# Loads for whole steps, one tile for a step's operands, and resident tiles of L in a layer of attention and RWKV-7 time mixing

## The chip, the cores and the metric

One core of a Trainium2 chip runs the whole layer. The metric is the device time of one launch in microseconds (us), the median of three runs. Engines are named as in the profile: PE (matrix engine), PEld (its weight load), DVE (vector), ACT (scalar), POOL (GpSimd), SP (the queue that issues every DMA here).

## The reference, cut to what matters

The layer normalises and modulates x, projects it once, gives half of the columns to eight heads of two-dimensional neighbourhood attention and half to eight heads of a bidirectional RWKV-7 recurrence, joins the two through an output projection, and ends in a SwiGLU feed-forward part. The recurrence is what the change touches:

```python
def wkv_scan(s0, r, w, k, v, a, b, reverse):
    '''S <- S diag(w) + (S a) b^T + v k^T ;  y = S r.'''
    def step(s, inp):
        r_t, w_t, k_t, v_t, a_t, b_t = inp
        sa = jnp.einsum('bhvk,bhk->bhv', s, a_t)
        s = s * w_t[:, :, None, :] + sa[..., None] * b_t[:, :, None, :] + v_t[..., None] * k_t[:, :, None, :]
        return s, jnp.einsum('bhvk,bhk->bhv', s, r_t)
...
    for d, rev in enumerate((False, True)):
        s_ctx, y_c = wkv_scan(s0, *ic, reverse=rev)
        _, y_x = wkv_scan(s_ctx, *ix, reverse=rev)
        wkv = wkv + y_x
...
        mix = jnp.concatenate([o_na, o_rw.astype(h.dtype)], axis=-1) @ w_out[l]
```

There are 2048 latent tokens in rows of 64, 256 context tokens, a width of 1024, and heads of 64.

## The kernel before

The program has three stages: projections (to about 895 us of the span), then the stage of this change, `phase2`, with the recurrence and the attention side by side (to about 1887 us), then the output projection (first matmul at L1458) and the feed-forward part.

**The recurrence in chunks.** The 2304 tokens are cut into 18 steps s of 128 tokens, each of two chunks of 64, so there are 36 chunks m = 2s + c. A chunk is worked for both directions and for four pairs of heads (hp or q) at once. Its operands (decayed keys, receptances and so on) were written to the DRAM tensor `d_b` by the stage before. Four kinds of work make a chunk ready:

- A *build* (L1004 to L1015), one per step and pair, loads `ga` and `bk`, multiplies them on PE, and copies or masks the product into `lx` (ACT, L1010), `ga` (DVE, L1011) and `gb` (DVE, L1015). `lx` holds the triangular matrices L.
- An *inverse*, one per two steps (a pair of steps, G = s // 2), inverts the triangles in `lx`. It is a long run of DVE operations on one tile (L1057 to L1089), then small matmuls and copies (L1104 to L1117).
- A *late* loads `bkl` and transposes it (L1028 to L1039), per chunk.
- A *load of v* fills `zv` (L1130), per chunk.

The *chain* then takes the chunks one after the other, since each needs the state z of the one before: copies of z into `zv` (L1175, L1176), matmuls with `ga` (L1185), a copy (L1189), matmuls with the inverted `lx` (L1195), copies (L1198, L1199), matmuls with `tt` (L1205), the new state on DVE (L1210, then L1225), and beside it the output y (L1218, L1222, L1230, stored to `d_y`).

**Attention** is 64 tiles: scores (L740), maxima and exponentials (L775 to L784, DVE and ACT), transposes (L790, L793), products (L829), a transpose back (L836) and the scaled output `ot` (L839). It shares no data with the recurrence.

**What sets the order.** Builds, inverses, lates, chain, attention and some preparation are generators ("streams"). `emit` merges them: it keeps a clock for each engine and always takes the piece that could start first, with the offsets of `LATE` (the tiles of attention come 60 us late, that is, last). The pieces say with "wait" and "post" what they need, and with "get" and "put" who holds the two PSUM banks that builds, lates, inverses and some of the preparation share. A scheduler then orders all instructions once more. Every engine, and SP, runs its instructions in the order that results.

**The waits that matter.** A build of pair G waits until the chain has done step 2G - 3, the last step of pair G - 2, since the tiles of `lx` come from two pools of one tile each. There are 16 units of `ga` and `gb`, one for each step and pair of heads, in a ring, so a build also waits for the step four before it. The inverse of G waits for the eight builds of steps 2G and 2G + 1, and the chain's step 2G waits for that inverse.

Of the kernel before, what the change touches and what calls it, by code (L numbers as in the profile page):

```python
# [19 lines left out]
P = 128  # L20
# [826 lines left out]
NU = 16  # L847
SHIFT = 1
# [9 lines left out]
LATE = (0, 0, -10, -10, 0, 0, 0, 60, 0)  # L858
# [3 lines left out]
def emit(banks, *streams):  # L862
# [4 lines left out]
    free, when = {}, {}  # L867
# [44 lines left out]
def phase2(k):  # L912
# [4 lines left out]
    with ExitStack() as ctx:  # L917
# [36 lines left out]
        U, LX, ZV, TT_ = {}, {}, {}, {}  # L954
# [4 lines left out]
        for i in range(NU):  # L959
            u = K()  # L960
            u.ga = un[i].tile([P, 3, 4, 64], F32, name=f"ga{i}")
            u.gb = un[i].tile([P, 2, 4, 64], F32, name=f"gb{i}")
# [8 lines left out]
        def build(s, hp, w):  # L971

            G, j0 = s // 2, 4 * (s % 2)
            u = units[(4 * s + hp + SHIFT) % NU]
# [4 lines left out]
            if G not in LX:  # L979
                LX[G] = lp[G % 2].tile([P, 4, 8, 64], F32, tag="lx", name="lx")  # L980
            lx = LX[G]
            U[s, hp] = u
            src = k.d_b[hp, s]
            for h in range(2):
                if s > 1:
                    nc.sync.dma_start(out=u.ga[H[h], h:3:2 - h], in_=src[H[h], 0:512].rearrange(
                        "p (x j t) -> p x j t", x=2, j=4))
                else:
                    nc.sync.dma_start(out=u.ga[H[h], h], in_=src[H[h], 0:256].rearrange("p (j t) -> p j t", j=4))
            bk = bp.tile([P, 4, 128], F32, tag=f"bk{w}", name="bk", bufs=2)  # L990
            nc.sync.dma_start(out=bk, in_=src[:, 512:1024].rearrange("p (j t) -> p j t", j=4))
            yield "run", ("DMA", 3.0)
# [8 lines left out]
            for j in range(4):  # L1001
                for h in range(2):
                    with run.next():
                        run.last = nc.tensor.matmul(gp[h][:, j, 0:N], bk[H[h], j], u.ga[H[h], h:3:2 - h, j, :] if s > 1  # L1004
                                                    else u.ga[H[h], h, j, :], start=True, stop=True).ins
            dc = "p (d c) t -> p d c t"
            for h in range(2):
# [3 lines left out]
                nc.vector.tensor_tensor(u.ga[ko, h].rearrange(dc, d=2), gp[h][ko, :, 0:64].rearrange(dc, d=2),  # L1011
                                        maskS[ko, :, None, :].to_broadcast([64, 2, 2, 64]), op=ALU.mult)
                if s > 1:
                    yield "run", ("DVE", -0.34)
                    nc.vector.tensor_tensor(u.gb[:, h].rearrange(dc, d=2), gp[h][:, :, 64:128].rearrange(dc, d=2),  # L1015
# [4 lines left out]
        def lates(g):  # L1020

            for m in range(2 * NS):
# [3 lines left out]
                bk = bl.tile([P, 2, 2, P], F32, tag="bkl", name="bkl")  # L1026
                for q in range(2):
# [3 lines left out]
                z = []  # L1031
                yield "get", z, 1
                yield "run", ("PE", 0.45)
                for q in range(2):
                    for dd in range(2):
                        nc.tensor.transpose(z[0][:, (2 * q + dd) * P:(2 * q + dd + 1) * P], bk[:, q, dd], k.ident)
                tt = TT_[m, g] = tp.tile([P, 2, 2, P], F32, tag=f"tt{g}", name="tt", bufs=2)
                yield "run", ("ACT", -0.52)
                nc.scalar.activation(tt.rearrange("p q d x -> p (q d x)"), z[0], AF.Copy)  # L1039
                yield "put", z[0]  # L1040
                yield "post", ("late", m, g)

        def inverses():
# [3 lines left out]
            for s in range(NS // 2):  # L1047
                yield ("wait",) + tuple(("built", 2 * s + e, hp) for e in range(2) for hp in range(4))
                lx = LX[s]
# [23 lines left out]
                for q in range(4, 32, 4):  # L1073

                    m, n = q, 32 - q
                    yield "run", ("DVE", 0.25 + 8 * m * n / 960)
# [45 lines left out]
        def load_v(m):  # L1122
# [3 lines left out]

            for h in range(2):
                for dd in range(2):
                    t0 = toks(s)[dd] + 64 * (1 - c if dd else c)
                    nc.sync.dma_start(out=zv[H[1 - h], h, dd, :], in_=k.d_vs[t0:t0 + 64, 256 * h:256 * h + 256])  # L1130
# [13 lines left out]
        def chains():  # L1144
# [5 lines left out]
            for s in range(NS):  # L1150
                yield "wait", ("inv", s // 2, 3)
                us = [U.pop((s, hp)) for hp in range(4)]
                for c in range(2):
                    m = 2 * s + c
                    yield "wait", ("late", m, 0), ("late", m, 1)
                    if m + 1 < 2 * NS:
                        load_v(m + 1)
                    z = yield from chain(s, c, z, us)
# [5 lines left out]
        def chain(s, c, z, us):  # L1164
            lx, j0 = LX[s // 2], 4 * (s % 2)
            zv = ZV[2 * s + c]
            tt = [TT_.pop((2 * s + c, g)) for g in range(2)]
# [14 lines left out]
            for i, (dd, q) in enumerate(dq):  # L1182
                for h in range(2):
                    with run.next():
                        run.last = nc.tensor.matmul(rp[H[h], i, :], us[q].ga[:, h, 2 * dd + c, :], slot(h, dd, q),  # L1185
# [522 lines left out]
```

## Time and profile before

| | |
|---|---|
| median of three runs | 3523.22 us (3523.1 to 3530.65) |
| profiled execution | 3522.23 us, its span 3520.5 us |
| mean granted clock of PE | 0.950 |
| PE busy over the span | 3239.0 us (92%) |
| DVE busy | 2396.8 us (68%) |
| ACT busy | 1465.8 us (42%) |

The shares are averages over three stages. Times in the text are microseconds from the start of the span of the profiled execution. Positions of the chain are given by the DVE operation at L1210, the new state z of a chunk: there are 36 of them, numbered from 0. The granted clock is a share of the full 2.4 GHz; 1.2 GHz is the other level.

### The profile page before, as it was taken

Reading aid. Unit: us, or ns where it says so; the run is one execution under the profiler, and the core shown is the slowest. Engines: PE = TensorE matmul, PEld = TensorE weight load, DVE = VectorE, ACT = ScalarE, POOL = GpSimd, SP = SyncE. Lnnn points to the kernel's source line nnn. Section 1 sums busy time; section 2 is a strip of 40 time slices with the busy share of each in tenths; the row PEclk is TensorE's granted clock in tenths of the full one; section 3 lists DMA queues with packets and bytes.
Section 4 is the critical chain, followed back from the end, with each engine's and each line's share of the span. In section 5 each row is a group of like instructions: output and inputs, shape, how many; then the busy total and the mean of one; then the engine's idle time right before and its main releaser. Section 6 shows DMA issues by size and latency. Waiting matters only on the chain. (4 is left out here: it accounts for less than half of the span.)

```text
span 3520.5 us, 66352 instructions
## 1 busy us (share of the span) xinstructions
PE 3239.0 (92%) x25202; PEld 2775.8 (79%) x25202; DVE 2396.8 (68%) x4489; ACT 1465.8 (42%) x3186; POOL 1101.2 (31%) x1057
## 2 busy tenths in 40 slices
PE   7899999999879889798856999999899999999999
PEld 5787878789657677576655887888799998899998
DVE  7758786774385766847655754444877778777776
ACT  4524343442445556465433553233333334333332
POOL 3425543453000100100113433333433334433332
PEclk9999999999888899899877999999999999999999
DMA  7546666553634446354326554332422223422222
GB/s 244 160 140 198 189 193 199 160 172 113 194 105 130 142 126 196 97 166 126 87 78 189 183 174 159 96 102 84 150 63 72 67 72 102 135 72 72 66 64 69
DMA packets 461856, 458.50 MB, mean 130 GB/s; under 512 B 56656, under 2 KB 381664, under 8 KB 461536
## 3 DMA queue, kind: packets, MB, share of 16 engines
q1 hardware_dynamic: 461536, 454.25, 42.7%
q8 instruction: 199, 3.26, 0.4%
q14 instruction: 121, 0.99, 0.1%
HBM read 346.37 MB, written 107.75 MB: 129 GB/s over the span
## 5 line engine op out<-in xcount | busy, mean ns | idle before, releaser
L1329 ACT ACTIVATE w<-raw 128x512 fp32r<-128x512 f32 x440 | 270.9, 627 | 497.8 <-PE acc L1618 190.2
L1538 PE MATMUL acc<-ua,w 128*128 128x384 f32 x2464 | 469.8, 336 | 6.0 <-POOL w L1330 2.7
L1618 PE MATMUL acc<-w,fh 128*128 128x512 f32 x1408 | 435.7, 394 | 18.7 <-ACT fh L1329 7.3
L1330 DVE TENSOR_TENSOR w<-raw,w 128x512 fp32r<-128x512 f32 x308 | 273.3, 891 | 247.0 <-ACT w L1329 120.0
L1538 PEld LDWEIGHTS acc<-ua,w 128*128 128x128 f32 x2464 | 433.2, 189 | 9.9 <-POOL w L1330 4.2
L219 PE MATMUL acc<-u,wh 128*128 128x512 f32 (+3 forms) x1120 | 347.9, 390 | 11.4 <-DVE sh L257 6.7
L1618 PEld LDWEIGHTS acc<-w,fh 128*128 128x128 f32 x1408 | 266.4, 190 | 79.4 <-ACT fh L1329 9.1
L503 PE MATMUL acc<-wt,u 128*128 128x256 f32 x2496 | 321.1, 287 | 5.0 <-DVE sh L257 2.3
L503 PEld LDWEIGHTS acc<-wt,u 128*128 128x128 f32 x2496 | 307.9, 194 | 12.3 <-issue 4.6
L1609 POOL TENSOR_TENSOR raw<-raw,gate 128x512 f32<-128x512 f32 x132 | 179.3, 1369 | 409.8 <-DMA raw<-in_w_dram 354.1
L1330 POOL TENSOR_TENSOR w<-raw,w 128x512 fp32r<-128x512 f32 x132 | 186.2, 1411 | 272.0 <-PE acc L1538 57.6
L1618 PE MATMUL acc<-w,fl 128*128 128x512 f32 x704 | 269.4, 392 | 0.1
L1538 PE MATMUL acc<-ux,w 128*128 128x384 f32 x1232 | 252.1, 335 | 0.3 <-DVE w L1330 0.3
L219 PEld LDWEIGHTS acc<-u,wh 128*128 128x128 f32 (+1 forms) x1120 | 206.0, 191 | 58.5 <-issue 7.0
L1520 PE MATMUL acc<-ua,w 128*128 128x512 f32 x1056 | 241.7, 389 | 2.0 <-POOL w L1330 1.1
L1520 PEld LDWEIGHTS acc<-ua,w 128*128 128x128 f32 x1056 | 198.0, 188 | 43.7 <-POOL w L1330 1.6
L219 PE MATMUL acc<-u,wl 128*128 128x512 f32 (+3 forms) x560 | 218.0, 389 | 2.8 <-DVE wl L210 2.7
L1538 PEld LDWEIGHTS acc<-ux,w 128*128 128x128 f32 x1232 | 216.8, 188 | 1.6 <-DVE w L1330 1.0
L1623 DVE TENSOR_TENSOR h<-h,acc 128x512 f32<-128x512 f32 x192 | 126.3, 683 | 100.3 <-PE acc L1618 100.1
L1179 POOL COPY zp<-z 64x512 f32<-64x512 f32 x64 | 41.4, 647 | 453.4 <-PE up L1218 293.7
L1330 POOL TENSOR_TENSOR w<-s,w 128x512 fp32r<-128x512 f32 x88 | 131.6, 1496 | 152.5 <-PE acc L1538 56.6
L1530 DVE TENSOR_TENSOR t<-acc,t 128x384 f32<-128x384 f32 x308 | 169.7, 551 | 13.9 <-PE acc L1538 7.3
(256 smaller groups left out, 6728.9 us busy)
## 6 DMA issues: line engine op xcount, KB each, us to landing
raw<-in_w_dram SPq DMA_DIRECT2D x132, 512.0 KB
raw<-in_w_dram SPq DMA_DIRECT2D x132, 256.0 KB
wada<-in_w_ada_dram SPq DMA_DIRECT2D x96, 256.0 KB
d_b<-bk SPq DMA_DIRECT2D x72, 256.0 KB
bkl<-d_b SPq DMA_DIRECT2D x144, 128.0 KB
bk<-d_b SPq DMA_DIRECT2D x72, 256.0 KB
d_b<-ar SPq DMA_DIRECT2D x136, 128.0 KB
xt<-in_x_dram SPq DMA_DIRECT2D x32, 512.0 KB
```

The lines of the kernel that those rows point to most:

```text
L219: nc.tensor.matmul(acc[:m, :n], a_[:, kk % 4, :m], b_[b][:, kk, :], start=(i == 0), stop=(i == 23))
L503: nc.tensor.matmul(acc[:, 256 * e:256 * e + 256], a_[b][:, kk, (j + e) * P:(j + e + 1) * P], ws[kk][:, h, :], start=(i == 0), stop=(i == 23))
L1179: nc.gpsimd.tensor_copy(zp[H[h], h], z[H[h]])
L1329: nc.scalar.activation(hl[0], v, AF.Copy)
L1330: eng.tensor_tensor(hl[1], v, hl[0].bitcast(F32), op=sub)
L1520: nc.tensor.matmul(acc, hl[wi][:, kk, :], u[ui][:, 4 * hf + kk, :], start=q == 0, stop=q == 23)
L1530: vadd = lambda o, x, y: nc.vector.tensor_tensor(o, x, y, op=add)
L1538: nc.tensor.matmul(acc, w[wi][:, kk, :], u[i][ui][:, kk, :], start=q == 0, stop=q == 11)
L1609: nc.gpsimd.tensor_tensor(raw, raw, g2[:, o], op=ALU.mult)
L1618: nc.tensor.matmul(acc, a_[:, f, ts], w2[f][:, hl, :], start=(i == 0), stop=(i == 6 * np_ - 1))
L1623: nc.vector.tensor_tensor(hs[j][:, o], hs[j][:, o], acc, op=add)
```

## The change

All of it is in `phase2` and `emit`.

- There are 4 units in place of 16, each for a whole step (all four pairs): `ga` is [128, 4, 3, 4, 64], `gb` is [128, 4, 2, 4, 64].
- A stream of builds loads for two pairs at a time: four DMAs for `ga` and one for `bk`, in place of four and two. The tile `bk` holds two pairs and has one buffer per stream (before, one pair and two buffers). The streams take pairs 0, 1 and 2, 3 (before 0, 2 and 1, 3).
- The two tiles of `lx` are made once and stay. The wait for step 2G - 3 is gone from the builds; what is left is the wait for step s - 4, before the loads of step s. So the first step of a pair can be built a step of the chain earlier; the second step still waits for 2G - 3.
- One stream of lates in place of two: two DMAs per chunk, each with all four pairs of one direction, in place of four; the two groups of transposes follow in turn.
- `zv` takes two DMAs per chunk, each with both directions, in place of four.
- In `emit`, a request for banks is served in the order in which it was made. The pieces of an inverse's DVE work are announced in larger blocks.

The number of instructions on PE, DVE, ACT and POOL is the same. There are 1963 DMAs in place of 2151. Lines of after are 1 to 6 higher than those of before for the same operation (L1057 is L1059, L1210 is L1216, L1225 is L1231, L1176 is L1182, L1458 is L1464); those of attention are unchanged.

```diff
-NU = 16
-SHIFT = 1
+NU = 4
-LATE = (0, 0, -10, -10, 0, 0, 0, 60, 0)
+LATE = (0, 0, -10, 0, 0, 0, 60, 0)
...
-                elif op == "get" and len(banks) >= args[1]:
+                elif op == "get" and e not in asked:
+                    asked.append(e)
+                    continue
+                elif op == "get" and asked[0] is e and len(banks) >= args[1]:
+                    asked.pop(0)
...
+        LX = [lp[i].tile([P, 4, 8, 64], F32, name=f"lx{i}") for i in range(2)]
...
             for s in range(NS):
-                for hp in (w, w + 2):
-                    yield from build(s, hp, w)
+                if s >= NU:
+                    yield "wait", ("chain", s - NU)
+                u = units[s % NU]
+                qs = slice(2 * w, 2 * w + 2)
+                src = k.d_b[qs, s]
+                for h in range(2):
+                    for x in range(2 if s > 1 else 1):
+                        nc.sync.dma_start(out=u.ga[H[h], qs, 2 if x else h].rearrange("p q j t -> p q (j t)"),
+                                          in_=src[:, H[h], 256 * x:256 * x + 256].rearrange("q p y -> p q y"))
+                bk = bp.tile([P, 2, 4, 128], F32, tag=f"bk{w}", name="bk")
+                nc.sync.dma_start(out=bk.rearrange("p q j t -> p q (j t)"),
+                                  in_=src[:, :, 512:1024].rearrange("q p y -> p q y"))
+                yield "run", ("DMA", 3.0)
+                for q in range(2):
+                    yield from build(s, 2 * w + q, u.ga[:, 2 * w + q], u.gb[:, 2 * w + q], bk[:, q])
...
-            if G > 1:
-                yield "wait", ("chain", 2 * G - 3)
-            if 4 * s + hp >= NU:
-                yield "wait", ("chain", (4 * s + hp - NU) // 4)
...
-                    nc.sync.dma_start(out=bk[:, q], in_=k.d_b[2 * g + q, s, :, 512:1024].rearrange(
-                        "p (d c x) -> c p d x", d=2, c=2)[c])
+                    nc.sync.dma_start(out=bk[:, :, dd], in_=k.d_b[:, s, :, x0:x0 + P].rearrange("q p x -> p q x"))
...
+                    if q % 2:
+                        yield "run", ("DVE", 1.0 if q == 1 else 4.2)
                     for i in range(q):
-                        yield "run", ("DVE", 0.5)
...
-                for dd in range(2):
-                    t0 = toks(s)[dd] + 64 * (1 - c if dd else c)
-                    nc.sync.dma_start(out=zv[H[1 - h], h, dd, :], in_=k.d_vs[t0:t0 + 64, 256 * h:256 * h + 256])
+                z = zv[H[1 - h], h]
+                nc.sync.dma_start(out=z if n0 < n1 else z[:, ::-1], in_=v[:, :, 256 * h:256 * h + 256])
...
-        emit(banks, chains(), inverses(), lates(0), lates(1), builds(0), builds(1), at.products(), at.tiles(),
+        emit(banks, chains(), inverses(), lates(), builds(0), builds(1), at.products(), at.tiles(),
```

**What it does to the order.** On DVE before, a middle inverse (G = 4; L1057 is its first operation) begins among builds and attention. At this place 16 chunks of the chain and 38 tiles of attention are done; no operation of the chain (L1176, L1199, L1210, L1225) stands on DVE between here and the inverse's last copy (L1117).

```order
L1011 TENSOR_TENSOR ga_9766<-bank_9724,maskS 64x256
L1015 TENSOR_TENSOR gb_9767<-bank_9724,maskI 128x256
L1057 STREAM_TRANSPOSE lu<-lx 128x32x32
L839 TENSOR_TENSOR ot<-sx_9781,st 128x128
L775 TENSOR_REDUCE st<-sx_9781 128x1
L1011 TENSOR_TENSOR ga_9764<-bank_9725,maskS 64x256
L1015 TENSOR_TENSOR gb_9765<-bank_9725,maskI 128x256
L1011 TENSOR_TENSOR ga_9764<-bank_9724,maskS 64x256
L1070 TENSOR_TENSOR xtmp<-lu 128x256
```

On DVE after, a middle inverse (G = 5; L1059 is its first operation) has the chain's operations (L1216 and L1231 the new state, L1182 the copy for the next chunk) among its own (L1073, L1075).

```order
L1059 STREAM_TRANSPOSE lu<-lx_9709 128x32x32
L1216 TENSOR_TENSOR z_15240<-rp,z_15010 128x512
L776 ISA pr,st<-sw_9720,es 128x384
L776 ISA st 128x1
L1231 TENSOR_TENSOR z_15240<-z_15240,pc 128x512
L778 TENSOR_SCALAR st<-st 128x1
L1073 TENSOR_TENSOR xtmp<-lu 128x256
L1182 COPY zv<-z_15240 64x512
L1075 TENSOR_TENSOR lu<-lu,xtmp 128x8x32
```

Between the two, chunks of the chain moved into the inverse: of the chunks done at the first and the last DVE operation of an inverse, before shows 8 and 8, 8 and 11, 16 and 16, 16 and 18, 24 and 24, 24 and 27, 32 and 32 for G = 2 to 8, and after 6 and 8, 9 and 12, 13 and 16, 17 and 20, 22 and 24, 25 and 28, 29 and 32.

On PE before, the chain's last matmuls (L1218, L1222, the output y) stand right ahead of the output projection (L1416 transposes its input, L1458 is its matmul); attention has ended long before.

```order
L1218 MATMUL up<-zp,ga_9758 64x64 x2
L1222 MATMUL up<-zv,gb_9759 64x64 x2
L1218 MATMUL up<-zp,ga_9760 64x64 x2
L1222 MATMUL up<-zv,gb_9761 64x64 x2
L1416 MATMUL mtp<-ident,mx 128x128 x4
L1458 MATMUL acc<-wo_20857,mh 128x512 x4
```

On PE after, the last rows ahead of the output projection (L1464) are those of attention (L793, L790, L829, L836); L1422 is the transposition of its input, L1285 a matmul of the time mixing's gate.

```order
L793 MATMUL sw_9721<-ident,pr 128x128 x3
L790 MATMUL sx_9722<-ident,pr 128x128 x2
L1422 MATMUL mtp<-ident,mx 128x128 x4
L836 MATMUL sx_9723<-ident,oT 128x128
L829 MATMUL sx_9722<-pr,vw 64x128 x6
L829 MATMUL sx_9722<-pr,vc 64x128 x4
L836 MATMUL sx_9723<-ident,oT 128x128
L1285 MATMUL g<-gup,gd 128x512
L1464 MATMUL acc<-wo_20482,mh 128x512 x3
```

The end of the chain moved ahead of the end of attention: after, 57 of the 64 outputs `ot` of attention stand ahead of the chain's last state z on DVE, before all 64.

On SP before, among the loads for a step are the two halves of `ga` (L986) of one pair each; L1028 loads half of a late.

```order
L1028 DMA bkl<-d_b 128x2x128 x2
L986 DMA ga_9750<-d_b 64x2x256
L986 DMA ga_9750<-d_b 64x512
L986 DMA ga_9752<-d_b 64x2x256
L986 DMA ga_9752<-d_b 64x512
```

On SP after, a load of `bk` (L984) or of `ga` (L981) carries two pairs, one of a late (L1030) four pairs, one of `zv` (L1136) both directions; `sg` is attention's.

```order
L1136 DMA zv<-d_vs 64x2x256 x2
L984 DMA bk<-d_b 128x2x512
L981 DMA ga_9710<-d_b 64x2x256 x2
L1030 DMA bkl<-d_b 128x4x128
L698 DMA sg<-d_k 128x8x128
L700 DMA sg<-d_q 128x4x128
L1030 DMA bkl<-d_b 128x4x128
```

The loads became fewer and larger, with the same bytes.

## Rows read from the trace of the kernel before

**Rows 1.** Windows: length, busy of PE, PEld, DVE, ACT, POOL, clock, DMA share, GB/s.
```profile
971.00:1091.00 120.00, 94.72 (x1293) 72.04 (x1289) 90.72 (x207) 53.38 (x139) 8.39 (x8) 0.78 0.36 102
1091.00:1786.00 695.00, 603.98 (x9313) 484.39 (x9311) 462.38 (x1182) 388.88 (x1027) 68.58 (x86) 0.91 0.48 136
1166.00:1249.00 83.00, 64.48 (x755) 47.56 (x750) 63.95 (x163) 41.17 (x115) 8.95 (x8) 0.86 0.38 109
1249.00:1382.00 133.00, 123.37 (x2130) 101.78 (x2130) 83.18 (x217) 84.65 (x223) 12.11 (x18) 0.95 0.59 164
1382.00:1464.00 82.00, 62.34 (x716) 47.93 (x715) 65.41 (x164) 38.94 (x107) 8.55 (x8) 0.84 0.40 117
```

**Rows 2.** Timeline of DVE: start, duration, operation; first inverse, states z, an inverse.
```profile
971.19 2.13 DVE L1057 STREAM_TRANSPOSE lu<-lx 128x1024 f32<-128x1024 f32 x1
...
1091.22 0.69 DVE L1210 TENSOR_TENSOR z<-rp,z 128x512 f32<-128x512 f32 x1 [1.47 <-PE rp L1205]
...
1302.48 0.69 DVE L1210 TENSOR_TENSOR z<-rp,z 128x512 f32<-128x512 f32 x1 [1.80 <-PE rp L1205]
...
1397.07 2.12 DVE L1057 STREAM_TRANSPOSE lu<-lx 128x1024 f32<-128x1024 f32 x1
...
1455.02 0.69 DVE L1117 COPY lx<-bank 32x512 f32<-32x512 f32 x1
...
1520.10 0.69 DVE L1210 TENSOR_TENSOR z<-rp,z 128x512 f32<-128x512 f32 x1 [1.22 <-PE rp L1205]
...
1785.60 0.67 DVE L1210 TENSOR_TENSOR z<-rp,z 128x512 f32<-128x512 f32 x1
```

**Rows 3.** Timeline of PE: first builds of steps 0, 8 and 9; the output projection begins.
```profile
909.36 0.69 PE L1004 MATMUL bank<-ga,bk 64*128 64x64 f32 x2
...
1310.44 0.83 PE L1004 MATMUL bank<-ga,bk 64*128 64x128 f32 x10
...
1349.91 1.16 PE L1004 MATMUL bank<-ga,bk 64*128 64x128 f32 x16
...
1886.91 1.08 PE L1416 MATMUL mtp<-ident,mx 128*128 128x128 f32 x4 [11.45 <-DMA mx<-d_mix]
1888.68 1.22 PE L1458 MATMUL acc<-wo,mh 128*128 128x512 f32 x2 [0.69 <-ACT mh L1329]
```

**Rows 4.** Groups of DVE, 1040 to 1834: count, busy, mean ns, idle before.
```profile
L1199 DVE COPY zv<-up 64x512 f32<-64x512 f32 x32 | 22.2, 695 | 26.9 <-ACT zv L1198 26.1
L1225 DVE TENSOR_TENSOR z<-z,pc 128x512 f32<-128x512 f32 x32 | 22.0, 687 | 0.4
L1210 DVE TENSOR_TENSOR z<-rp,z 128x512 f32<-128x512 f32 x32 | 21.9, 684 | 21.4 <-PE rp L1205 21.4
...
L1176 DVE COPY zv<-z 64x512 f32<-64x512 f32 x32 | 16.0, 500 | 1.0
```

**Rows 5.** Groups of PE that are attention's, 1091 to 1786, columns as in rows 4.
```profile
L740 PE MATMUL sw<-ks,q 64*128 64x384 f32 (+1 forms) x200 | 76.2, 618 | 1.9 <-ACT pr L798 1.8
L740 PE MATMUL sx<-kc,q 64*128 64x256 f32 x198 | 69.5, 433 | 2.0 <-ACT pr L796 2.0
...
L793 PE MATMUL sw<-ident,pr 128*128 128x128 f32 x348 | 60.4, 299 | 12.9 <-ACT pr L784 12.5
L829 PE MATMUL sx<-pr,vw 128*64 128x128 f32 x708 | 56.9, 288 | 8.3 <-ACT pr L782 4.1 <-DVE st L775 3.4 <-ACT pr L796 0.6
...
L790 PE MATMUL sx<-ident,pr 128*128 128x128 f32 x200 | 40.7, 307 | 3.6 <-ACT pr L782 3.3
...
L829 PE MATMUL sx<-pr,vc 128*64 128x128 f32 x408 | 36.6, 278 | 0.0
...
L836 PE MATMUL sx<-ident,oT 128*128 128x128 f32 x51 | 16.4, 321 | 2.7 <-ACT oT L834 2.6
```

**Rows 6.** Loads of the lates: issue time in ns, and who waited (us, times).
```profile
L1028 SPq DMA_DIRECT2D bkl<-d_b x144: 354/468/1443, 859.0 to 1832.0; - x144
...
  PE bank L1036: 13.4, 8
```

More of the change, by code (lines that the diff above doesn't have):

```diff
@@ L967, in builds, with build @@
             for s in range(NS):
-                for hp in (w, w + 2):
-                    yield from build(s, hp, w)
-        def build(s, hp, w):
-            G, j0 = s // 2, 4 * (s % 2)
-            u = units[(4 * s + hp + SHIFT) % NU]
-            if G > 1:
-                yield "wait", ("chain", 2 * G - 3)
-            if 4 * s + hp >= NU:
-                yield "wait", ("chain", (4 * s + hp - NU) // 4)
[L979 to L992, printed above, removed]
+                if s >= NU:
[13 more added lines that the diff above has]
+                    yield from build(s, 2 * w + q, u.ga[:, 2 * w + q], u.gb[:, 2 * w + q], bk[:, q])
+        def build(s, hp, ga, gb, bk):
+            G, j0 = s // 2, 4 * (s % 2)
+            lx = LX[G % 2]
             N = 128 if s > 1 else 64
@@ L1075, in inverses @@
                     m, n = q, 32 - q
-                    yield "run", ("DVE", 0.25 + 8 * m * n / 960)
+                    if q % 8 == 4:
+                        yield "run", ("DVE", sum(0.25 + 8 * r * (32 - r) / 960 for r in (q, q + 4) if r < 32))
                     tv = tmp[:, :4 * m * n].rearrange("p (c a b) -> p a c b", c=4, a=m)
@@ L1151, in chains @@
                 yield "wait", ("inv", s // 2, 3)
-                us = [U.pop((s, hp)) for hp in range(4)]
+                u = units[s % NU]
                 for c in range(2):
                     m = 2 * s + c
-                    yield "wait", ("late", m, 0), ("late", m, 1)
+                    yield "wait", ("late", m)
                     if m + 1 < 2 * NS:
                         load_v(m + 1)
-                    z = yield from chain(s, c, z, us)
+                    z = yield from chain(s, c, z, u)
                     yield "post", ("chunk", m)
@@ L1162, in phase2, with chain @@
         dq = [(dd, q) for dd in range(2) for q in range(4)]
-        def chain(s, c, z, us):
-            lx, j0 = LX[s // 2], 4 * (s % 2)
+        def chain(s, c, z, u):
+            lx, j0 = LX[s // 2 % 2], 4 * (s % 2)
             zv = ZV[2 * s + c]
-            tt = [TT_.pop((2 * s + c, g)) for g in range(2)]
+            tt = TT_.pop(2 * s + c)
             zf = z.rearrange("p d q n -> p d (q n)")
@@ L1184, in chain @@
                     with run.next():
-                        run.last = nc.tensor.matmul(rp[H[h], i, :], us[q].ga[:, h, 2 * dd + c, :], slot(h, dd, q),
+                        run.last = nc.tensor.matmul(rp[H[h], i, :], u.ga[:, q, h, 2 * dd + c, :], slot(h, dd, q),
                                                     start=True, stop=True).ins
@@ L1204, in chain @@
                     with run.next():
-                        run.last = nc.tensor.matmul(rp[H[h], i, :], tt[q // 2][:, q % 2, dd, H[h]], slot(h, dd, q),
+                        run.last = nc.tensor.matmul(rp[H[h], i, :], tt[:, q, dd, H[h]], slot(h, dd, q),
                                                     start=True, stop=True).ins
@@ L1217, in chain @@
                         with run.next():
[L1218 removed]
+                            run.last = nc.tensor.matmul(up_[H[h], i, :], u.ga[:, q, 2, 2 * dd + c, :],
                                                         zp[:, h, dd, q, :], start=True, stop=False).ins
@@ L1221, in chain @@
                         with run.next():
-                            run.last = nc.tensor.matmul(up_[H[h], i, :], us[q].gb[:, h, 2 * dd + c, :],
+                            run.last = nc.tensor.matmul(up_[H[h], i, :], u.gb[:, q, h, 2 * dd + c, :],
                                                         slot(h, dd, q), start=False, stop=True).ins
```

52 lines of the change are left out of this document (28 added, 24 removed).

## The prediction

> **What bounds the kernel now.** The change touches one stage, so I read that stage alone, first by its windows, then by the position of the chain. From the state z of chunk 3 at 1091.22 us to that of chunk 31 at 1785.60 us [rows 2] the stage is in its steady course: PE is busy 603.98 of 695 us (87%), DVE 462.38 (67%), ACT 388.88 (56%) [rows 1]. No engine is full, and yet nothing idles for long. The three windows behind it in that group show why: the course swings between two conditions. From 1249 to 1382 PE is busy 123.37 of 133 us (93%) and DVE 83.18 (63%). Just before it and just after it, in 1166 to 1249 and 1382 to 1464, PE is at 78% and 76%, DVE at 77% and 80%, and the granted clock falls from 0.95 to 0.86 and 0.84. These are the stretches in which the chain stands and two inverses run one behind the other on DVE.
>
> The chain shows the loop that makes them. The state of chunk 11 (end of step 5) comes at 1302.48. Only then may builds of steps 8 and 9 begin; on PE they start at 1310.44 and 1349.91 [rows 3]. The inverse of that pair starts on DVE at 1397.07 and its last copy begins at 1455.02 [rows 2]. So 94.6 us pass from the chain to the inverse, 58.6 in the inverse (to the end of its 0.69 us copy), and four chunks then run in 64.4, until 1520.10. The sum is 217.6 us for eight chunks. From 1091.22 to 1785.60 there are 28 chunks in 694.4 us, or 99.2 us for four. I call the time of four chunks p.
>
> **The change part by part.** The sum is made against the profiled execution, 3522.2 us, which lies 1.0 under the median.
>
> *Start, to the state of chunk 3.* After, all eight builds of the first two steps stand ahead of attention's first scores, so inverse 0 needs only them. Before, the first build is at 909.36 [rows 3] and the inverse begins at 971.19 [rows 2]. Sixteen matmul records of a build, all it has, lie within 1.16 us on PE [rows 3], and with the turn of two banks through ACT and DVE I estimate 3 us for each, 24 for eight; a first build at about 903 and 8 us to the inverse's first operation give 935, or 36 earlier. But what stands on DVE from there to the state of chunk 3 grows: by counts of the order times the mean durations of before, from 101 to 119 us. At the packing of 971 to 1091, where DVE is busy 90.72 of 120 us [rows 1], that is 120 × 119 / 101 = 141, so 21 are given back. **Net 15 gained**, with bounds 0 and 30.
>
> *Steady course, 28 chunks: 7p.* The loop gets shorter by the first of its two steps of builds, since the first step of a pair now waits for step 2G - 4: 94.6 less the 39.5 between 1310.44 and 1349.91 [rows 3] leaves 55.1. The inverse gets longer, as three chunks of the chain now run within it: four DVE operations of 0.695, 0.687, 0.684 and 0.500 us [rows 4] are 2.57 us a chunk, 7.7 for three, so 66.3. With 64.4 for four free chunks the eight take 185.8, so p = 93. From the other side, PE: 603.98 us of work done at a clock of 0.91, of which the part in the two standing stretches ran at 0.84 to 0.86. At 0.95 those would shrink by a tenth, and over the whole I take 590. At the 93% of the best window that is 634, or p = 91. **I take p = 92**, 644 us in place of 694.4: 50 gained. For this, PE and DVE must be busy together for (590 + 462) / 644 = 163% of the time, where the three windows show 155, 155 and 156% and the whole 153%. This is what I trust least: bounds are p = 86 (PE shrinks to 565 at 94%) and 99.2 (no better packing).
>
> *End, from the state of chunk 31 to the output projection.* Before this is 1785.60 to 1888.68 [rows 2, 3], 103.1 us: inverse 8 and four chunks alone, without attention, which is done. After, about 18 us of inverse 8's DVE work is left at that point, which I put at 19 us, then come four chunks with five tiles of attention, at the pace of four free chunks, 65. Then seven tiles of attention are left alone. On PE a tile costs at least 7.1 us: the seven groups sum to 356.7 over the 50 tiles of that window (200 sw records, four to a tile) [rows 5]. At most it costs 13.9, the 695 us of the window by 50. Alone it is nearer to the first; I take 8, so 56 us. The idle 11.45 us of PE for the last input [rows 3] is covered, since time mixing of the first tiles now lies beside attention, but the splits of the output weights come after the last tile, which I put at 4 us, under those 11.45. Together 144, **41 lost**, with bounds 28 and 82.
>
> *Loads.* 188 DMAs fewer, with an issue of 0.468 us for one of a late [rows 6], are some 88 us of SP. SP is not what others wait for: PE waited 13.4 us in all for such loads [rows 6]. One load for two pairs with a single `bk` buffer comes later than one for a pair, and the loads of the second step of a pair still start only when the chain is through. Bounds are 13 gained and, if each of the seven pairs waits 4 us longer, 28 lost; I take 0, since the lates and `zv` have chunks of lead. The Trainium skill ("DMA: Bandwidth & Descriptors", Rules for kernel authors) says to coalesce many small transfers; its section on the anatomy of one DMA gives about 2.0 us fixed for each on another path than this one. By that, an estimate from the page, 188 would be 376 us and the time 3122 if they lay on the path; rows 6 speak against that. The same rules say that two transfers to disjoint partition halves serialize, which speaks against the halves that `ga` and `zv` keep; no row here separates that.
>
> *FIFO of the banks, larger blocks, fewer units.* They only move the order, and that is counted above. Instruction counts of the four computing engines do not change.
>
> The sum: 15 + (694.4 - 7p) - 41 = 668 - 7p. With p = 92 it is 24 us gained: **3522.2 - 24 = 3498 us**, 3499 against the median. A measurement here can tell about 0.3%, 10.6 us, from no change. So the change is faster below p = 94.0, the same to 97.0, and slower above.
>
> **The rivals.**
>
> *Better packing.* With the inverses beside the chain nothing stands, PE stays at its 93% or above and the clock at 0.95. For it: the 1249 to 1382 window held that for 133 us, with DVE at 63%. Against it: DVE must carry 77% at the same time, which no PE-bound window here shows. At p = 86 the gain is 66, 3456 us.
>
> *No change.* p = 95.5, so that the end's 41 us eat the middle: 3522. It happens if DVE, at 77 to 80% in the standing stretches, keeps the chain's operations waiting about 1 us a chunk more than I took, or if the later loads cost their 4 us a pair.
>
> *Slower: the inverse in the chain's way.* DVE runs in order. In an inverse of after, an operation of the chain stands behind a run of inverse operations, and PE and ACT, which have the chunk's next matmuls and copies in their own order, stand behind it with attention's work queued up. Before, the chain simply stood there and attention filled PE. If each of three chunks waits 2 us at each of its three hops to DVE, 18 us, the loop is 203.8 for eight chunks, p = 102, and the time is 3522 - 668 + 714 = 3568. If the pace merely stays at 99.2, the end alone makes it 3548. From p = 97 it decides. For it: 21.4 and 26.9 us of DVE idle before L1210 and L1199 [rows 4] show that these hops wait on PE and ACT, so a shift at one comes out at the others. Against it: the chain has few DVE operations, and work beside it fills in.
>
> *The change doesn't do what it says.* The order shows the chain's rows inside the inverses, so this is left with next to nothing.
>
> **How the numbers follow.** I give the forecast (p from 88 to 94) 0.45, better packing (p under 88) 0.15, no change 0.17, slower 0.23. So faster by over 0.3% is 0.60, within 0.3% is 0.17, slower by over 0.3% is 0.23. The range leaves out about 2 in 10: below, p = 86 with 4 us of the other bounds, 3452; above, p = 99.2 to 99.5, 3550. The likeliest case alone reaches from 3470 to 3512.
>
> **What would show it right or wrong.** In the profile after: the first inverse (L1059) at about 935; the state of chunk 3 (L1216) near 1076; from there to chunk 31 some 644 us, with PE near 90%, DVE near 72% and a clock that no longer dips to 0.85; no stretch of 70 us in which the chain stands; about 144 us from chunk 31 to the first L1464, with some 56 us at a lower clock that only attention fills. If 28 chunks take over 680 us, packing was the wrong step; if the end takes over 160, the tiles alone were sized wrongly; if PE waits for `bk` or `ga` from DMA for over 20 us, the loads were.

## The result and the profile after

The changed kernel takes 3493.83 us (median of six, 3486.9 to 3511.09) against 3524.22 (3521.88 to 3532.28) for the kernel before beside it: a ratio of 0.9915, with a 95% interval of 0.9895 to 0.9936. It is faster by 30 us; the forecast was 3498 us. The profiled executions are 3492.62 and 3522.23 us, 29.6 apart. The landmarks of after that answer to [rows 2] and [rows 3] are these, from the timelines of DVE and PE (start, duration, operation): the first inverse, states z of chunks 3, 11, 15, 19, 23, 31 and 35 (L1216), two middle inverses (L1059 to L1121) and the last one's end, the first build and the first output projection.

```profile
932.67 2.12 DVE L1059 STREAM_TRANSPOSE lu<-lx 128x1024 f32<-128x1024 f32 x1
...
1072.80 0.67 DVE L1216 TENSOR_TENSOR z<-rp,z 128x512 f32<-128x512 f32 x1
...
1244.25 0.68 DVE L1216 TENSOR_TENSOR z<-rp,z 128x512 f32<-128x512 f32 x1
...
1300.69 2.08 DVE L1059 STREAM_TRANSPOSE lu<-lx 128x1024 f32<-128x1024 f32 x1
...
1352.26 0.69 DVE L1216 TENSOR_TENSOR z<-rp,z 128x512 f32<-128x512 f32 x1
...
1366.86 0.69 DVE L1121 COPY lx<-bank 32x512 f32<-32x512 f32 x1
...
1393.36 2.15 DVE L1059 STREAM_TRANSPOSE lu<-lx 128x1024 f32<-128x1024 f32 x1
...
1433.58 0.69 DVE L1216 TENSOR_TENSOR z<-rp,z 128x512 f32<-128x512 f32 x1 [1.57 <-PE rp L1211]
...
1471.20 0.69 DVE L1121 COPY lx<-bank 32x512 f32<-32x512 f32 x1 [2.47 <-ACT lx L1121]
...
1535.39 0.69 DVE L1216 TENSOR_TENSOR z<-rp,z 128x512 f32<-128x512 f32 x1 [0.71 <-PE rp L1211]
...
1728.48 0.68 DVE L1216 TENSOR_TENSOR z<-rp,z 128x512 f32<-128x512 f32 x1
...
1751.83 0.69 DVE L1121 COPY lx<-bank 32x512 f32<-32x512 f32 x1 [0.74 <-ACT lx L1121]
...
1803.67 0.69 DVE L1216 TENSOR_TENSOR z<-rp,z 128x512 f32<-128x512 f32 x1 [0.98 <-PE rp L1211]
```

```profile
890.50 0.43 PE L1005 MATMUL bank<-ga,bk 64*128 64x64 f32 x2
...
1856.06 1.03 PE L1285 MATMUL g<-gup,gd 128*128 128x512 f32 x2
1856.84 0.73 PE L1464 MATMUL acc<-wo,mh 128*128 128x512 f32 x2
```

The windows (columns as in [rows 1]) of the steady course, of one inverse within it, and of the attention that is left behind the chain:

```profile
1072.80:1728.50 655.70, 580.13 (x8993) 464.09 (x8992) 459.37 (x1125) 356.12 (x922) 74.57 (x89) 0.90 0.51 141
...
1393.00:1472.00 79.00, 65.17 (x1008) 51.73 (x1004) 54.21 (x129) 37.54 (x101) 7.16 (x9) 0.83 0.52 143
...
1804.00:1857.00 53.00, 41.92 (x326) 26.78 (x323) 28.16 (x87) 28.71 (x86) 15.17 (x12) 0.90 0.50 155
```

Read term by term against [rows 2, 3]:

| stretch | before | after | gained | forecast |
|---|---|---|---|---|
| to the state of chunk 3 | 1091.2 | 1072.8 | 18.4 | 15 |
| 28 chunks, to chunk 31 | 694.4 | 655.7 | 38.7 | 50 |
| chunk 31 to the output projection | 103.1 | 128.4 | -25.3 | -41 |
| the rest | 1631.8 | 1634.1 | -2.3 | 0 |

So the three terms have the sign and roughly the size of the sum, and their errors (3 us of gain too little, 11 too much, 16 of loss too much) cancel to 5 us, which is luck. Work also moved between the stretches: of the 64 tiles of attention, before does 13 ahead of the state of chunk 3 and 51 in the 28 chunks; after does 8 and 44, and the other 12 after chunk 31, five of them beside the last four chunks and seven alone. So a term that shrank may only have handed on its work. The change also moves the wait, the order of the banks, the blocks of an inverse and the loads at once. The experiments take them apart.

### The profile page after: what moved, and what is told of

The parts are those of the page before. It is cut to its first block, busy times and chain, and to the rows that moved or that the text cites. A ratio compares the mean times of both kernels' runs of the same rounds, so it can differ in the third digit from the quotient of the medians.

```text
span 3490.9 us, 66140 instructions
## 1 busy us (share of the span) xinstructions
PE 3265.8 (94%) x25202; PEld 2788.0 (80%) x25202; DVE 2396.7 (69%) x4489; ACT 1466.9 (42%) x3186; POOL 1107.7 (32%) x1057
## 5 line engine op out<-in xcount | busy, mean ns | idle before, releaser
L1544 PEld LDWEIGHTS acc<-ux,w 128*128 128x128 f32 x1232 | 216.8, 188 | 3.0 <-POOL w L1336 1.5
```

The lines of the kernel that those rows point to most:

```text
L1544: nc.tensor.matmul(acc, w[wi][:, kk, :], u[i][ui][:, kk, :], start=q == 0, stop=q == 11)
```

## The experiments

Three theories stood at the start: A, the loop is shorter because the wait for step 2G - 3 is gone (the prediction's); B, the new order of the requests for banks does it; C, the fewer DMAs do it. Ratios are always to the kernel before on the same chip. "28 chunks" runs from the state z of chunk 3 to that of chunk 31, the "end" from there to the first output projection, both in the one profiled execution. The tiles are outputs `ot` of attention on DVE within the 28 chunks, of 64 in all; before has 51 there, after 44.

| label | what it is | median us | ratio (95%) | 28 chunks, tiles | end |
|---|---|---|---|---|---|
| e1_wait_back | after, old wait | 3502.24 | 0.9914 (0.9888 to 0.9941) | 701.5, 52 | 98.4 |
| e2_small_loads | after, small loads | 3490.77 | 0.9878 (0.9860 to 0.9897) | 652.8, 44 | 130.4 |
| e3_banks_as_before | after, old bank order and blocks | 3502.65 | 0.9910 (0.9888 to 0.9932) | 684.3, 50 | 90.3 |
| e4_resident_L_alone | before, resident L, no wait | 3485.46 | 0.9866 (0.9844 to 0.9888) | 654.2, 50 | 95.5 |
| e5_changed_again | after | 3500.85 | 0.9915 (0.9899 to 0.9931) | 650.8, 44 | 133.7 |
| e6_resident_L_again | as e4 | 3486.03 | 0.9870 (0.9848 to 0.9892) | 659.1, 50 | 97.2 |
| e7_bank_order_alone | before, new bank order | 3494.44 | 0.9895 (0.9877 to 0.9914) | 701.2, 53 | 105.4 |
| e8_small_blocks | after, small blocks | 3469.79 | 0.9836 (0.9810 to 0.9862) | 669.0, 48 | 92.9 |
| e9_small_blocks_again | as e8 | 3470.46 | 0.9831 (0.9811 to 0.9852) | 670.7, 48 | 95.4 |
| e10_small_blocks_small_loads | e8 with small loads | 3465.14 | 0.9815 (0.9792 to 0.9837) | 666.8, 48 | 98.7 |
| e11_large_loads_alone | before, new loads, units and lates | 3517.16 | 0.9961 (0.9947 to 0.9975) | 687.7, 51 | 102.7 |
| e12_resident_L_large_blocks | e4 with large blocks | 3502.86 | 0.9915 (0.9890 to 0.9939) | 691.5, 47 | 83.4 |

Kernels e1 to e4 ran beside each other, e5 to e8, and e9 to e12; the kernel before had medians of 3536.33, 3530.95 and 3530.95 there.

**The old wait back in the changed kernel.**

```diff
                 if s >= NU:
-                    yield "wait", ("chain", s - NU)
+                    yield "wait", ("chain", s // 2 * 2 - 3)
```

> The changed kernel with the old wait put back: the loads and builds of both steps of a pair G wait for the chain's step 2G - 3 again. Theory A (my prediction: the loop is shorter because the first step of a pair is built a step earlier): the 28 chunks from chunk 3 to chunk 31 go back from 656 us towards 694, and the time to 3515 or above. Theory B (the gain comes from the order in which the two shared banks are given out, which lets inverses and chain run side by side): the 28 chunks stay under 675 us and the time between 3475 and 3500; the order shows all 64 tiles of attention ahead of the chain's last state, so the end is short. Theory C (fewer and larger DMAs): 3494 as in the changed kernel.

The middle is as long as theory A says: 701.5 us where after needs 655.7. Its window, and the timeline of the same execution at the states of chunks 3 and 31 and at the output projection:

```profile
1074.50:1776.00 701.50, 635.72 (x9444) 503.94 (x9442) 477.71 (x1221) 404.76 (x1057) 72.16 (x89) 0.91 0.51 141
```

```profile
1074.53 0.69 DVE L1216 TENSOR_TENSOR z<-rp,z 128x512 f32<-128x512 f32 x1 [1.45 <-PE rp L1211]
...
1776.01 0.68 DVE L1216 TENSOR_TENSOR z<-rp,z 128x512 f32<-128x512 f32 x1
```

```profile
1874.42 0.79 PE L1464 MATMUL acc<-wo,mh 128*128 128x512 f32 x1 [0.69 <-ACT mh L1335]
```

But the time does not. PE carries 55.6 us more work in this middle (635.72 against 580.13), eight tiles of attention that after leaves to the end, and the end is 30 us shorter. So the longer middle does not show what the wait costs: the eight tiles lengthen it too. (The profiled execution is the longest of its four, 11 us above their median.) Against the kernel before the ratio is that of the changed kernel: in this kernel, removing the wait is worth nothing that these runs can tell, which by the two intervals is some 12 us either way. Theory A missed here in the total.

**Small loads in the changed kernel.**

```diff
-                        nc.sync.dma_start(out=u.ga[H[h], qs, 2 if x else h]...
+                        for q in range(2):
+                            nc.sync.dma_start(out=u.ga[H[h], 2 * w + q, 2 if x else h]...
...
-                nc.sync.dma_start(out=bk.rearrange("p q j t -> p q (j t)"), ...
+                for q in range(2):
+                    nc.sync.dma_start(out=bk[:, q].rearrange("p j t -> p (j t)"), in_=src[q, :, 512:1024])
...
-                    nc.sync.dma_start(out=bk[:, :, dd], ...
+                    for q in range(0, 4, 2):
+                        nc.sync.dma_start(out=bk[:, q:q + 2, dd], ...
...
-                nc.sync.dma_start(out=z if n0 < n1 else z[:, ::-1], in_=v[:, :, 256 * h:256 * h + 256])
+                for dd, n in enumerate((n0, n1)):
+                    nc.sync.dma_start(out=zv[H[1 - h], h, dd, :], in_=k.d_vs[64 * n:64 * n + 64, 256 * h:256 * h + 256])
```

> The changed kernel with its loads cut again into the sizes of the kernel before (one pair for each load of ga and bk, two pairs for bkl, one direction for zv), 188 DMAs more. The order on DVE has the same chunks and tiles at each inverse. Theories A and B: 3494, within 10 us, and at most 15 us of PE waiting for DMA more. Theory C (fewer and larger DMAs): most of the 30 us gained is gone, 3515 or above.

The experiment goes further than its expectation says. The kernel before loads `ga` of two pairs with four DMAs of 128 KB for most steps, and the changed kernel does the same; only the other loads were merged. Cutting `ga` by pairs too makes 272 loads of 64 KB out of 136, so this kernel has 316 DMAs more than the changed one, 128 more than the kernel before, and not 188. It takes 3490.77 us: even so nothing of the gain is lost. The window of its 28 chunks is after's within 3 us. Theory C falls for the changed kernel.

```profile
1076.90:1729.70 652.80, 577.57 (x8992) 460.01 (x8993) 459.54 (x1125) 357.80 (x922) 72.70 (x89) 0.91 0.50 142
```

**Banks and blocks as before in the changed kernel, and the wait's removal alone in the kernel before.** The first has, in `emit` and `inverses`, the old lines again, and the copy of a late is announced with 0.52 in place of 0.6, as before:

```diff
-                elif op == "get" and e not in asked:
-                    asked.append(e)
-                    continue
-                elif op == "get" and asked[0] is e and len(banks) >= args[1]:
-                    asked.pop(0)
+                elif op == "get" and len(banks) >= args[1]:
...
-                    if q % 2:
-                        yield "run", ("DVE", 1.0 if q == 1 else 4.2)
                     for i in range(q):
+                        yield "run", ("DVE", 0.5)
...
-                    if q % 8 == 4:
-                        yield "run", ("DVE", sum(0.25 + 8 * r * (32 - r) / 960 for r in (q, q + 4) if r < 32))
+                    yield "run", ("DVE", 0.25 + 8 * m * n / 960)
```

> The changed kernel with the old rule of emit: a bank goes to whichever stream asks first in the walk, not in the order of the requests, and an inverse is announced in its old small blocks. Resident tiles of L, units and large loads stay. Theory A: the wait is gone, so the 28 chunks take about 656 us and the time is 3494 or less. Theory B: the chain stands at every second pair again for some 70 us, 28 chunks in 680 us or more, 3515 or above. Theory C: 3494.

The second is the kernel before with one part of the change, the resident tiles and with them no wait:

```diff
+        LX = [lp[i].tile([P, 4, 8, 64], F32, name=f"lx{i}") for i in range(2)]
...
-            if G > 1:
-                yield "wait", ("chain", 2 * G - 3)
...
-            if G not in LX:
-                LX[G] = lp[G % 2].tile([P, 4, 8, 64], F32, tag="lx", name="lx")
-            lx = LX[G]
+            lx = LX[G % 2]
```

> The kernel before with one part of the change alone: two tiles of L that stay, and no wait for step 2G - 3. Loads, units and the rule for the banks as before. Theory A: the loop of eight chunks is 30 to 40 us shorter, the 28 chunks take 600 to 660 us, 3460 to 3500. Theory B: the order still lets the chain stand at every second pair, 3510 to 3530. Theory C: 3524.

e3 answers neither theory: 684.3 us for 28 chunks is B's size, 0.991 is A's. e4 is clear. The wait's removal alone takes 1.3% off the kernel before, more than the whole change does, with the chain still standing at every second pair (71, 76 and 74 us from one state to the next, at chunks 8, 16 and 24, where before has 100, 100 and 97). So these three steps are 75 us shorter together and the other 25 are 35 longer: what attention did while the chain stood now runs beside the chunks. e6 repeats the ratio (0.9870), with 659.1 us for the 28 chunks. (The profiled execution of e4 is the shortest of its four, 11 us below their median.) Its window and landmarks:

```profile
1087.60:1741.80 654.20, 583.41 (x9266) 472.69 (x9268) 462.88 (x1175) 385.47 (x1015) 71.48 (x89) 0.93 0.51 143
```

```profile
1087.58 0.69 DVE L1207 TENSOR_TENSOR z<-rp,z 128x512 f32<-128x512 f32 x1
...
1741.80 0.69 DVE L1207 TENSOR_TENSOR z<-rp,z 128x512 f32<-128x512 f32 x1 [0.46 <-PE rp L1202]
```

DVE has the work of before in it (462.88 against 462.38 us, [rows 1]) and 50 of before's 51 tiles, in 40 us less. So the shorter loop is a gain of the prediction's kind, shown where nothing else changes.

The traces also show where e3 loses it. The first build of step 8 may start once the chain has done step 4, that is chunk 9. The states of chunk 9 and the first builds of step 8 in e4 and in e3:

```profile
1232.23 0.69 DVE L1207 TENSOR_TENSOR z<-rp,z 128x512 f32<-128x512 f32 x1
...
1239.11 1.51 PE L1001 MATMUL bank<-ga,bk 64*128 64x128 f32 x16 [1.63 <-DMA ga<-d_b]
```

```profile
1264.91 0.68 DVE L1210 TENSOR_TENSOR z<-rp,z 128x512 f32<-128x512 f32 x1
...
1296.19 0.49 PE L1001 MATMUL bank<-ga,bk 64*128 64x128 f32 x2
```

In e4 the build follows after 6.9 us, in e3 after 31.3, and so it is at steps 4, 12 and 16 (0 to 6 us in e4, 26 to 32 in e3). What e3 gained by the missing wait its order gives back ahead of the build. Why it stands there so late was not tried.

**The two kernels side by side, and the new bank order alone.** From here on theory D: the wait's removal makes the gain of the middle, and what came with it pushes seven tiles of attention behind the chain.

> The changed kernel itself, as the measure for the three beside it on this chip: 0.9915 of the kernel before, within 0.003.

> The kernel before with resident tiles of L and without the wait for step 2G - 3, the rest as before, once more and beside the changed kernel. If the gain of the steady course is that of the wait alone and the bank order only pushes seven tiles of attention behind the chain (theory D, formed after the first four runs), this is faster than the changed kernel by 7 to 20 us: 28 chunks in 654 us, the end in 95. If its one profile was a lucky one (rival), both agree within 5 us.

> The kernel before with the order of the requests for the banks alone; wait, loads, units and blocks as before. All 64 outputs of attention stand ahead of the last state. Theory D: the start is 15 to 20 us shorter, the 28 chunks stay at 690 or more because the wait is there, the end at about 100: 3500 to 3515. Rival (the bank order makes the steady course): 28 chunks under 670, below 3490.

e5 repeats the changed kernel's ratio. e6 is faster than it by 15 us (3486.03 against 3500.85), inside theory D's 7 to 20. e7 adds to the kernel before only the lines of `emit` that serve the banks in the order of the requests: 3494.44, better than the 3500 to 3515 expected, since the start gives 33 us and not 15 to 20. The state of chunk 3 comes at 1058.64 in place of 1091.22 [rows 2]; its 28 chunks are not shorter (701 us, with 53 tiles).

```profile
1058.64 0.69 DVE L1214 TENSOR_TENSOR z<-rp,z 128x512 f32<-128x512 f32 x1 [0.65 <-PE rp L1209]
...
1759.83 0.69 DVE L1214 TENSOR_TENSOR z<-rp,z 128x512 f32<-128x512 f32 x1 [0.53 <-PE rp L1209]
```

So the bank order is worth 1.05% by itself, and by another stretch than the wait: the start. But the start is not only quicker, it holds less: 8 tiles of attention stand ahead of the state of chunk 3 in place of 13. From the last matmul of the projections to that state, in the kernel before and in e7:

```profile
893.60:1091.20 197.60, 158.43 (x1835) 120.40 (x1833) 124.57 (x318) 97.00 (x265) 11.86 (x12) 0.81 0.51 144
```

```profile
897.50:1058.60 161.10, 131.52 (x1595) 102.66 (x1592) 109.97 (x261) 75.54 (x196) 11.90 (x12) 0.77 0.52 148
```

The stretch is 36.5 us shorter, and PE does 27 us less in it. The gain of the whole comes about because the five tiles find room later: the 28 chunks take 7 us more with two of them, the end 2 us more with three.

**Small blocks of an inverse in the changed kernel.** The diff is the second half of that of e3, and the copy of a late is announced with 0.52 in place of 0.6 again.

> The changed kernel with an inverse announced in its old small blocks, all else kept. The order leaves one tile of attention behind the chain in place of seven. If the seven tiles alone are what the end costs and the middle had room for them (theory D1): the end falls from 128 to about 95 us, the 28 chunks grow by less than 15, 3465 to 3480. If PE is the bound of the middle (theory D2): six tiles of 7.1 us come back there, 28 chunks in 690 or more, 3490 to 3500.

3469.79 us, 31 below the changed kernel on the same chip: the fastest so far, theory D1. One tile is left behind the chain in place of seven, and the end falls from 133.7 (e5) to 92.9.

```profile
1069.00:1738.00 669.00, 591.92 (x9306) 472.54 (x9306) 481.24 (x1189) 383.26 (x995) 73.39 (x90) 0.93 0.53 144
```

```profile
1830.82 1.65 PE L1462 MATMUL acc<-wo,mh 128*128 128x512 f32 x3 [0.69 <-ACT mh L1333]
```

The 28 chunks hold four tiles more and take 18 us longer than e5's, a little over the 15 that D1 allowed (13 against the first profile of after). The engines are together busy (591.92 + 481.24) / 669 = 160% of the time, against 158.5% in after and 153% before [rows 1]. DVE does 22 us more in 13 us more than in after.

**The last four: loads with small blocks, loads alone, and blocks without the bank order.**

> The changed kernel with small blocks of an inverse once more, as the measure for the next one on this chip: 0.984 of the kernel before, within 0.003.

> The same with the loads cut into the sizes of before, 188 DMAs more. If the size of the loads is worth nothing either way (my term of 0): within 8 us of the kernel with large loads beside it. If large loads that come later cost (theory L, after 0.9878 with small loads against 0.9915 with large ones on other chips): 8 to 15 us faster. If fewer DMAs help: 8 us or more slower.

e8 repeats (e9: 3470.46). With the small loads of e2 (e10, again 316 DMAs more and not 188) it is 3465.14, 5 us lower with overlapping intervals: the size of the loads is worth nothing that can be told here, as the term of 0 said. e10 is the fastest version of the study by its median.

> The kernel before with the loads, units and the single stream of lates of the changed one, and nothing else: the wait for step 2G - 3 is there, the banks and blocks as before. With my term of 0: 0.997 to 1.003 of the kernel before. Theory L: slower by 8 us or more. If fewer DMAs help: 0.995 or below.

Here neither 0 nor theory L holds: 0.9961, about 14 us gained (9 to 19 by the interval). The kernel before does profit a little from the large loads, units and the single stream of lates together; which of the three is open, since they also shift the order. This kernel was made from the changed one, so it also keeps the two resident tiles, with the wait in force. It differs from e3 by the wait alone: removing it there takes 0.9961 to 0.9910, and the 28 chunks from 687.7 to 684.3 only.

> The kernel before with resident tiles of L, no wait for step 2G - 3, and an inverse announced in large blocks; banks and loads as before. All 64 outputs of attention stand ahead of the last state. If large blocks cost only by pushing attention behind the chain (which needs the bank order too): like resident L alone, 0.984 to 0.990. If they hold up the chain by themselves: 28 chunks 15 us or more above the 654 to 659 of resident L alone, 0.990 to 0.998.

0.9915, where resident L alone has 0.987: large blocks cost some 0.45% by themselves, without the bank order and with all 64 tiles ahead of the chain's last state (the intervals just touch, on different chips). Of its 28 chunks (with 47 tiles) the window says

```profile
1079.70:1771.20 691.50, 614.85 (x9458) 491.32 (x9459) 470.04 (x1185) 385.04 (x996) 72.23 (x89) 0.91 0.49 138
```

which is 37 us more than e4's, while the end is 12 shorter. So the blocks do hold up the course itself. The tail of seven tiles needs three things at once: no wait, the bank order and the large blocks. With any one of them missing (e1, e12, e8) none or one tile is left behind the chain's last state.

## Why the prediction was right, point by point

**Start.** The inverse was put at 935 and starts at 932.67; the state of chunk 3 at 1076, it is 1072.80. The first build was put at about 903 and comes at 890.50. e7 shows that this gain is the bank order's: with it alone the start shortens by 33 us, and e3, without it, has the state of chunk 3 at 1085.05. I had ascribed it to the order without saying what made it. Two errors cancel in it: from the first build to the inverse I took 32 us and it took 42.2. And I did not count that five tiles of attention leave the start; they come back in the end.

**Steady course by the loop.** The mechanism is there: the first build of step 8 starts 8.4 us after the state of chunk 9, which stands ahead of chunk 11, on which it waited before ([rows 2, 3]).

```profile
1209.65 0.68 DVE L1216 TENSOR_TENSOR z<-rp,z 128x512 f32<-128x512 f32 x1
...
1218.08 1.19 PE L1005 MATMUL bank<-ga,bk 64*128 64x128 f32 x6 [4.13 <-issue]
```

The loop's three parts were put at 55.1, 66.3 and 64.4, together 185.8. From the rows above, the cycle that I had read (chunks 11 to 19) has 1300.69 - 1244.25 = 56.4 to the inverse, 66.9 in it (to the end of the last copy), and 66.0 for four chunks: 189.3. The next (15 to 23) has 41.1, 78.5 and 63.5: 183.1. But these two are the best of five. The others, 7 to 15, 19 to 27 and 23 to 31, take 216.8, 203.7 and 193.1. Cut by the states of chunks 3, 7, 15, 23 and 31, the stretch is

| chunks | before | after | tiles before, after | e4 |
|---|---|---|---|---|
| 3 to 7 | 65.6 | 62.6 | 6, 5 | 59.8 |
| 7 to 15 | 213.5 | 216.8 | 16, 13 | 196.9 |
| 15 to 23 | 220.8 | 183.1 | 17, 12 | 206.5 |
| 23 to 31 | 194.6 | 193.1 | 12, 14 | 191.1 |

The windows of 7 to 15 and 15 to 23, before and then after:

```profile
1156.80:1370.30 213.50, 185.35 (x2857) 147.47 (x2855) 147.60 (x379) 122.34 (x331) 21.06 (x26) 0.91 0.52 144
1370.30:1591.00 220.70, 189.51 (x2870) 151.98 (x2869) 147.58 (x380) 125.48 (x334) 21.30 (x26) 0.91 0.51 145
```

```profile
1135.40:1352.30 216.90, 187.81 (x2831) 147.79 (x2828) 157.01 (x376) 115.57 (x295) 24.43 (x28) 0.87 0.52 142
1352.30:1535.40 183.10, 158.09 (x2468) 127.30 (x2468) 126.47 (x312) 96.25 (x250) 18.86 (x24) 0.90 0.52 142
```

So a cycle of eight takes 197.7 us on average in after and 209.6 before: 12 us are gained and not the 31.8 forecast, and nearly all of it lies in one cycle, 15 to 23, which holds five tiles less. e5 has the same pattern (211.7, 183.6, 192.8). The 28 chunks come near 7p because the first four run free, in 62.6 us, and I had counted them at p like the rest; that is luck. That the wait governs the loop is shown by e4, where it alone is removed and the work stays, and there too a cycle gains 11 us. e1 does not show it, because eight tiles came back into its middle.

**Steady course by the engines.** Here the working failed, and the result hid it. I took the engines' work of the 28 chunks before, 590 and 462 us, for after as well, and charged seven tiles once more in the end. They are the same tiles: after has 44 in this stretch, before 51. Counted once, seven tiles of 7.1 us [rows 5] off the 590 leave 540, and at 93% PE's bound would have been 581 us, p = 83, not 91. The two roads to p agreed only by that mistake. PE measured 580.13, more than 540. In part that is its clock, which did not rise: 0.90 where I expected 0.95, and 0.83 in the inverse of 1393 to 1472. By the 603.98 us at 0.91 of [rows 1], less seven tiles, 554 would be left, 560 at 0.90; the other 20 us are open, and 7.1 for a tile that lies among other work is itself an estimate. Packing came to 158.5%, not 163%. "The clock no longer dips" was wrong.

**End.** Sized at 144, it measured 128.4: 24.0 from chunk 31 to the end of the inverse's last copy (19 forecast), 51.2 for four chunks with five tiles (65 forecast, from four chunks in a run stretch, too slow by 14), 53.2 from chunk 35 to the output projection for seven tiles and the splits of weights (60 forecast). The clock in that stretch was 0.90. The mechanism is confirmed by e8, where six of the seven tiles go back beside the chain and the end shrinks by 41 us.

**Loads.** The term was 0, between 13 gained and 28 lost. In the changed kernel PE's waits for loads of the lates fell from 13.4 us [rows 6] to 5.7, and one wait of 4.1 for `bk` came up, at 916.6, in the builds. From the views of L1030 (who waited for it) and of L1005 (what it waited for):

```profile
L1030 SPq DMA_DIRECT2D bkl<-d_b x72: 359/505/1572, 855.6 to 1762.7; - x72
...
  PE bank L1039: 5.7, 3
```

```profile
  DMA bk<-d_b: 4.1, 1
```

e2 against after and e10 against e9 agree with 0. In e11, 188 DMAs fewer came with about 14 us, 0.07 us each, with the units and the single stream of lates in the same sum. The Trainium skill's fixed cost of about 2.0 us per DMA ("DMA: Bandwidth & Descriptors", the section on the anatomy of one DMA) is given for DMAs that GpSimd issues, and here SP issues all of them, so no run here measures it.

**The rival that decided part of it.** "The inverse in the chain's way" did not make the kernel slower, but it is there. Five of after's six middle inverses take 72 to 79 us against 55 to 60 before. In one of them DVE stands for 2.86 us at an attention output, with the rest of an inverse's block (L1085, L1086) and the chain's copy (L1205) in its queue behind it:

```profile
1217.14 0.96 DVE L1082 TENSOR_TENSOR xtmp<-lu 128x768 f32<-128x768 f32 x1
1220.96 0.29 DVE L839 TENSOR_TENSOR ot<-sx,st 128x128 f32<-128x128 f32 x1 [2.86 <-PE sx L836]
1221.28 0.43 DVE L1012 TENSOR_TENSOR ga<-bank,maskS 64x256 f32<-64x256 f32 x1
1221.72 0.42 DVE L1016 TENSOR_TENSOR gb<-bank,maskI 128x256 f32<-128x256 f32 x1
1222.07 0.55 DVE L1085 TENSOR_TENSOR xtmp<-xtmp 128x384 f32<-128x384 f32 x1
...
1223.91 0.69 DVE L1205 COPY zv<-up 64x512 f32<-64x512 f32 x1 [0.37 <-ACT zv L1204]
```

**What the parts are worth.** Alone, on the kernel before: the wait 1.3%, the bank order 1.05%, the loads, units and single late stream 0.4%. All parts but the large blocks: 1.65%. With the large blocks: 0.85%. So the change leaves about half of its gain in the announcement of the inverse's blocks. The parts do not add up: the wait's removal is worth 1.3% on the kernel before (e4, e6), 0.5% with the new loads and units (e3 against e11), and nothing that shows within the changed kernel (e1), where the middle and the end trade 46 against 30 us in the profiles. The changed kernel with its wait, its small loads or its old bank order and blocks back (e1, e2, e3) keeps a ratio of 0.988 to 0.991, so no one of these makes its 30 us, and the sum of the prediction, which gave the wait 50 of them, came out right in part by luck. Why the parts eat each other's gain stays open.

## What to carry to other kernels

Before counting what a stretch gains, count what work it still holds: work that moved to a later stretch must leave the first when it is charged in the second. When a change of several parts wins a little, take out each part alone; here one part, the large blocks, cost as much as the change won. And where a loop of builds, an inverse and a chain sets the pace, the time from the last use of a buffer to its refill is the place to look, and how the filler work is placed at the end decides what of the gain is kept.

## What was not expected of the hardware

The granted clock of PE was not simply higher where PE was busier. What sets it here was not tried; these are the rows. In the 28 chunks it is 0.91 before [rows 1] with PE busy 87% and 0.90 after with 88%; 0.93 in e4 and e8 with 89% and 88%. In after's inverse of 1393 to 1472, with PE 82% busy, it is 0.83, and in the 53 us of attention alone, with PE 79% busy, 0.90.
